# Group norm sums as four column tiles, the inverse's two products interleaved, and one block's attention pushed later

## The chip, the cores and the metric

One core of a Trainium2 chip runs the kernel. The metric is device time in microseconds (us), the median of three runs. TensorE (PE in the profile) does the matrix products, VectorE (DVE) and ScalarE (ACT) the elementwise work, GpSimd (POOL) a few fills; SyncE's queue (SP) starts nearly all transfers.

## What is computed

One layer of a decoder over 2048 prompt tokens and 64 sample tokens, width 1024. Two branches read the same normed input: sliding-window attention, and an RWKV-7 time mixer with a 64x64 state per head. Their outputs are gated, summed and projected, and a convolutional FFN follows. The two pieces that matter here:

```python
# per head of 64 channels, at every token
mean = jnp.mean(y, axis=-1, keepdims=True)
var = jnp.mean(jnp.square(y - mean), axis=-1, keepdims=True)
y = (y - mean) * lax.rsqrt(var + LNX_EPS)
...
sa = jnp.einsum('bhij,bhj->bhi', S, at)
S = S * wt[:, :, None, :] + sa[..., None] * bt[:, :, None, :] + vt[..., None] * kt[:, :, None, :]
```

The second is a recurrence over tokens. The kernel does it in chunks of 64 tokens; inside a chunk a unit triangular 64x64 system is solved, for which `inverse` builds the inverse of its matrix out of 32x32 blocks: the two diagonal blocks by substitution on VectorE, the corner block by two products, first `g`, then `g` times a diagonal block.

## The kernel before

The 2112 tokens are cut into three blocks of 704, and each block into two halves of 384 and 320 tokens. For each block: the input projection (with preparation of the recurrence), attention, inverses, chunk recurrence with group norm, then `branches` (the two output projections), `merge` (the mixing projection and the sum of squares of the next norm), and `ffn_stage`. The projection of all three blocks comes first, then branches, merge and FFN of block 0, of block 1 and of block 2.

All the large products go through `mm3` (L348 to L355): float32 values are split into a high and a low part, and three float32r products of 128x128 weights with 384 or 320 columns are added up. Below, one such product is called a *wide product*. Before every third wide product `mm3` calls `tick`, which may run one step of a background generator. The generators stand in named queues; queue "c" holds attention, inverses, chunks (recurrence and group norm) and the gathering of the branch inputs (`gather`), strictly one after the other. A generator yields how long its next step should wait, by costs written into the kernel (`cost`, `account`). `drain("c")` runs what is left in the queue. Within all this a list scheduler of the compiler still moves instructions on an engine; the rows of the section on the change show what it made of them. PE runs its instructions in that order.

The queue's contents before: attention of block 0 during the projection of block 0, inverses of block 0 during that of block 1, chunks of block 0 during that of block 2. Then

```python
self.push("c", self.attention(1), self.attention(2), self.inverses(1), self.chunks(1))
```

at branches, merge and FFN of block 0 (L1702), and inverses and chunks of block 2 at those of block 1 (L1729 to L1730), each with a drain at the end of the FFN. Sample attention belongs to block 2's.

At a group norm (`groupnorm`, L1237) four tiles `y` (two heads of 64 channels each, 384 tokens) are centred by L367, squared into `gsq`, and `headsum` (L997) sums the squares per head: twelve products (four tiles, three groups of 128 tokens), each with 128x128 squares as the weights and a two-column constant as the moving operand, so that each gives two columns. Every float32 product is two records of the trace. `merge` ends with a norm over channels: `rowsums` (L416, one-column products), a few small VectorE steps (L423, L375 to L380), and three transposes (L1037 on `nwyd`), emitted at the latest after the first 24 wide products of the FFN.

Of the kernel before, what the change touches and what calls it, by code (L numbers as in the profile page):

```python
# [14 lines left out]
ALU = mybir.AluOpType  # L15
# [15 lines left out]
LNX = 64e-5  # L31
# [12 lines left out]

CST = {}
_n = 0
for _name, _w in (("ident", 128), ("maskp", 128), ("sel", 2), ("selm", 2), ("ones", 1), ("bm", 8),
                  ("cj", 128), ("blk", 128), ("m65", 390), ("att", 256), ("masks", 128), ("m65s", 332)):
    CST[_name] = (_n, _w)
    _n += _w  # L50
# [3 lines left out]
def constants():  # L54
    c = np.zeros((P, NCST), np.float32)

    def put(name, a):
        o, w = CST[name]
        c[:, o:o + w] = a

    i = np.arange(P)
    put("ident", np.eye(P))
    s, t = i[:, None] % 64, i[None, :] % 64
    late = (i[None, :] >= 64)
    causal = np.where(late, s <= t, s < t)
    put("maskp", causal)
    put("masks", causal & (s // 8 == t // 8))
    head = (i[:, None] // 64 == np.arange(2)[None, :])
    put("sel", head)
    put("selm", head / 64.0)  # L70
    put("ones", 1.0)
    same = (i[:, None] // 64 == i[None, :] // 64)
    put("cj", np.eye(P) - same / 64.0)
    put("blk", same)
    d = 128 + i[:, None] - np.arange(256)[None, :]
    put("att", np.where((d >= 0) & (d <= 128), 0.0, NEG))
    m = np.ones(390, np.float32)
# [23 lines left out]
class Kernel:  # L101
# [892 lines left out]
            return self.tp.tile([P, 2, 384], F32, tag="xv", name="kt", bufs=2)[:].rearrange("p a c -> p (a c)")[:, :512].rearrange("p (c j) -> p c j", j=128)  # L994
        return pp.tile([P, 4, 128], F32, tag="m", name=name, bufs=2)

    def headsum(self, sq, sel, least, eps, k):  # L997

        nc = self.nc
        nt = 3 * len(sq)  # L1000
        ps = self.bank(k)
        for t in range(nt):
            nc.tensor.matmul(ps[:, 2 * t:2 * t + 2], sq[t // 3][:, t % 3 * 128:(t % 3 + 1) * 128], self.cst(sel),  # L1003
                             start=True, stop=True)
        m = self.small(2 * nt, "hsm" + k)
        if eps is None:
            nc.vector.tensor_scalar(m, ps[:, :2 * nt], least, None, op0=ALU.max)
        else:
            nc.vector.tensor_scalar(m, ps[:, :2 * nt], eps, None, op0=ALU.add)
        return self.rsqrt(m, 2 * nt, k)  # L1010

    def headrow(self, rb, r, t0):
# [6 lines left out]
    def keynorm(self, p, xk, pp):  # L1019

        nc = self.nc
        sq = [self.ntmp("nsq") for _ in HALF]
        for t, (c0, n) in zip(sq, HALF):
            nc.scalar.activation(t[:, :n], xk[:, c0:c0 + n], ACT.Square, scale=self.par("k_k", p))
        nc.gpsimd.memset(sq[1][:, HALF[1][1]:], 1.0)
        yield 0.2
        r = self.headsum(sq, "sel", 1e-24, None, "r")
        rb = pp.tile([P, 6, 128], F32, tag="rbk", name="rbk", bufs=2)
        self.headrow(rb, r, 0)
        yield 0.2  # L1030
        self.rbk[p] = rb
# [8 lines left out]
    def inverse(self, b, hf, ip):  # L1040


        nc = self.nc
        nch = HALF[hf][1] // 64
        ns = 4 * nch

        def blocks(rows, r, cols):
            for p in range(4):
                nc.sync.dma_start(t0[rows, p * nch:(p + 1) * nch],
                                  self.md[b][hf][:nch, rows, p, r, cols].rearrange("c q j -> q c j"))  # L1050

# [24 lines left out]
        q = ip.tile([P, 32, 64], F32, tag="qi", name="qinv")  # L1076
        t1 = ip.tile([P, 32, 32], F32, tag="nb", name="t1")
        nc.vector.transpose(t1[:].rearrange("p b i -> p i b"), qb[:].rearrange("p t i -> p i t"))
        yield
        nc.vector.transpose(q[:, :, 32:].rearrange("p b t -> p t b"), qb)  # L1080
        for r in range(2):
            o = 64 - r * 64
            nc.scalar.copy(q[o:o + 32, :ns, :32], q[o:o + 32, :ns, 32:])
            nc.gpsimd.memset(q[o + 32:o + 64, :, 0:32], 0.0)
        g = ip.tile([P, 24, 32], F32, tag="qb", name="g")
        yield 0.3
        for u in range(0, ns, 16):
            k = min(16, ns - u)
            ps = self.bank()
            for c in range(k):  # L1090
                for r in range(2):
                    o = 64 - r * 64
                    nc.tensor.matmul(ps[o + 32:o + 64, c * 32:(c + 1) * 32], n12[o:o + 32, u + c], t1[o:o + 32, u + c],
                                     start=True, stop=True)
            for r in range(2):
                rows = slice(96 - r * 64, 128 - r * 64)
                nc.scalar.copy(g[rows, u:u + k].rearrange("p c j -> p (c j)"), ps[rows, :k * 32])
            yield 0.2
            ps = self.bank()
            for c in range(k):  # L1100
                for r in range(2):
                    o = 64 - r * 64
                    nc.tensor.matmul(ps[o:o + 32, c * 32:(c + 1) * 32], g[o + 32:o + 64, u + c],
                                     q[o + 32:o + 64, u + c, 32:64], start=True, stop=True)
            for r in range(2):
                rows = slice(64 - r * 64, 96 - r * 64)
                nc.scalar.copy(q[rows, u:u + k, 32:64], ps[rows, :k * 32].rearrange("p (c j) -> p c j", j=32))
            yield
        for p in range(4):
            nc.sync.dma_start(self.qqd[b][hf][:nch, :, p].rearrange("c q j -> q c j"), q[:, p * nch:(p + 1) * nch])  # L1110

# [125 lines left out]
    def groupnorm(self, b, hf, y, kp, gup, gs):  # L1237

        nc = self.nc
        c0, n = HALF[hf]  # L1240
        sq = kp.tile([P, 4, 384], F32, tag="gsq", name="gsq", bufs=1)
# [4 lines left out]
        t, ready = part(0)  # L1246
        for p in range(4):
            nxt = part(p + 1) if bufs == 2 and p < 3 else None
            yield (ready,)
            ps = self.spread("cj", t, n, "c")  # L1250
# [3 lines left out]
            if p < 3:  # L1254
                yield (0.0,)
                t, ready = nxt or part(p + 1)
        yield (last,)
        r = self.headsum([sq[:, p] for p in range(4)], "selm", None, LNX, "c")

        def row(p):  # L1260
            rb = kp.tile([P, 3, 128], F32, tag="grb", name="grb", bufs=bufs)
# [6 lines left out]
        for p in range(4):  # L1268
# [6 lines left out]
            ps = self.bank("c")  # L1275
# [351 lines left out]
    def attention(self, b):  # L1627
        with self.pool("att", side="right") as ap:
            yield from self.attn_prompt(b, ap)
            if b == NB - 1:  # L1630
                yield from self.attn_sample(ap)

    def inverses(self, b):
        with self.pool("inv", side="right") as ip:
            for hf in range(2):
                yield from self.together((1.4, [self.inverse(b, hf, ip)]))
# [35 lines left out]
    def run(self):  # L1672
        self.sts, self.ols = {}, deque()
        HOLD = 4
        hs = ExitStack()
# [19 lines left out]
        with self.pool("gt") as gp:  # L1695
# [3 lines left out]
            self.drain("c")  # L1699
            lp[0].__exit__(None, None, None)  # L1700
            hs.close()
            self.push("c", self.attention(1), self.attention(2), self.inverses(1), self.chunks(1))  # L1702
            with self.pool("ms") as mp:
                ms = self.bigtile(mp, "o")
                self.branches(0, os_, ms, gts, x)
# [1 line left out]
        for b in (1, 2):  # L1707
# [16 lines left out]
            with ExitStack() as ms_:  # L1724
                mp = old if b == 2 else ms_.enter_context(self.pool("ms"))
                ms = self.bigtile(mp, "o")
                self.branches(b, os_, ms, gts, x)
                gp.__exit__(None, None, None)
                if b == 1:  # L1729
                    self.push("c", self.inverses(2), self.chunks(2))  # L1730
                xs = self.merge(b, x, ms, xp, op)
        self.ffn_stage(2, *xs, old)
        es.close()
# [83 lines left out]
```

## Time and profile before

| | us |
|---|---|
| median of 3 runs (3223.59 to 3227.27) | 3224.35 |
| the profiled execution, its own time | 3225.91 |
| span of the profiled execution | 3224.1 |
| PE busy in the span | 3195.1 (99%) |
| DVE busy | 2033.0 (63%) |
| ACT busy | 1216.3 (38%) |

The span runs from the first to the last instruction; some 1.8 us of the execution lie around it. The profiled execution is 1.56 us above the median. Starts of matmul records are measured, their ends are modelled; so a stretch on PE is best read from the start of its first record to the start of what follows.

### The profile page before, as it was taken

What the parts mean: (1) busy time and instruction counts of PE and PEld (TensorE: products, weight loads), DVE (VectorE), ACT (ScalarE), POOL (GpSimd) and SP (SyncE); (2) the same over time, 40 slices, a digit from 0 to 9 for tenths busy, and PEclk for the clock granted to TensorE, in tenths of its full rate; (3) what the DMA queues carried; (4) which work ended last, traced back from release to release, by engine and by line L of the source; (5) the groups of instructions that cost most, each with busy time, mean ns of one, the idle gap of its engine ahead of it and who ended that gap; (6) DMA issues with size and microseconds to landing.
All of it is one profiled execution on the core that took longest, in us unless ns stands there. A gap on an engine that the chain in (4) does not pass through costs nothing.

```text
span 3224.1 us, 60163 instructions
## 1 busy us (share of the span) xinstructions
PE 3195.1 (99%) x24072; PEld 3082.8 (96%) x24072; DVE 2033.0 (63%) x4601; ACT 1216.3 (38%) x2272; POOL 34.7 (1%) x99
## 2 busy tenths in 40 slices
PE   8999999999999999999999999999999999999998
PEld 8999999999999998899999999999999999999998
DVE  7676677745655576677555678855566575555556
ACT  4455433343323575633222333332223333222232
POOL 0000000000000000000000000000000000000000
PEclk9999999999999999999999999999999999999999
DMA  4644454545655633322443373253324362212222
GB/s 154 190 140 127 131 160 142 145 139 163 189 178 169 219 108 99 97 74 79 137 130 123 115 237 110 76 176 114 115 72 134 112 215 83 72 66 73 66 71 73
DMA packets 335464, 408.79 MB, mean 127 GB/s; under 512 B 110928, under 2 KB 261456, under 8 KB 334928
## 3 DMA queue, kind: packets, MB, share of 16 engines
q1 hardware_dynamic: 330576, 399.17, 39.7%
q10 hardware_dynamic: 4608, 5.77, 0.5%
q8 instruction: 189, 3.10, 0.4%
q14 instruction: 91, 0.75, 0.1%
HBM read 307.41 MB, written 98.41 MB: 126 GB/s over the span
## 4 chain that ended last, share of the span: by engine, by line
PE 82%; issue 16%; DVE 1%; DMA 0%; ACT 0%; POOL 0%; SPq 0%; POOLq 0%; DVEq 0%
PE psd L354 70%; PE psr L976 2%; PE psr L679 1%; PE psr L727 1%; PE psr L714 1%; PE psc L1184 1%; PE psr L866 1%; PE psc L1144 1%; PE psc L1177 1%; PE psc L1003 0%; PE psr L1003 0%; PE psr L964 0%; PE psc L1187 0%; PE psc L1276 0%; PE psr L354 0%
## 5 line engine op out<-in xcount | busy, mean ns | idle before, releaser
L354 PE MATMUL psd<-o,wp 128*128 128x320 f32 (+1 forms) x8736 | 1457.4, 325 | 1.3 <-DVE x L1458 1.0
L354 PEld LDWEIGHTS psd<-o,wp 128*128 128x128 f32 x8736 | 1404.4, 188 | 14.0 <-issue 4.2
L354 PE MATMUL psd<-h,wp 128*128 128x320 f32 (+1 forms) x5112 | 895.4, 328 | 11.2 <-ACT wp L340 7.7
L354 PEld LDWEIGHTS psd<-h,wp 128*128 128x128 f32 x5112 | 824.8, 189 | 23.5 <-ACT wp L340 7.7
L340 ACT CAST wp<-wr 128x1024 fp32r<-128x1024 f32 x350 | 366.9, 1048 | 602.9 <-PE psd L354 567.6
L341 DVE TENSOR_TENSOR wp<-wr,wp 128x1024 fp32r<-128x1024 f32 x350 | 428.1, 1223 | 166.8 <-ACT wp L340 161.0
L354 PE MATMUL psd<-ff,wp 128*128 128x320 f32 (+1 forms) x2880 | 489.1, 327 | 2.1 <-DVE up L1423 1.2
L354 PEld LDWEIGHTS psd<-ff,wp 128*128 128x128 f32 x2880 | 468.0, 189 | 7.7 <-issue 1.6
L1458 DVE TENSOR_TENSOR x<-x,psd 128x384 f32<-128x384 f32 (+1 forms) x288 | 148.0, 519 | 204.4 <-PE psd L354 203.5
L1430 DVE TENSOR_TENSOR gb<-psd,rb 128x64 f32<-128x64 f32 (+2 forms) x154 | 70.6, 471 | 194.9 <-PE psd L354 192.4
L1431 ACT ACTIVATE cc<-gb,pt 128x64 f32<-128x64 f32 (+2 forms) x154 | 95.6, 636 | 181.9 <-DVE gb L1430 180.3
L1433 DVE SCALAR_TENSOR_TENSOR cc<-gb,pt,cc 128x704 f32<-128x704 f32 (+1 forms) x132 | 122.0, 924 | 2.7 <-ACT cc L1431 2.0
L1442 ACT ACTIVATE cc<-cc 128x704 f32<-128x704 f32 x66 | 52.3, 793 | 142.8 <-DVE cc L1433 88.2
L1423 DVE TENSOR_TENSOR up<-psd,rb 128x384 f32<-128x384 f32 (+1 forms) x132 | 68.9, 522 | 50.4 <-PE psd L354 49.9
L1294 ACT ACTIVATE g<-psd,der 128x384 f32<-128x384 f32 (+1 forms) x64 | 35.4, 554 | 150.0 <-PE psd L354 98.7
L345 ACT CAST ff<-cc 128x384 fp32r<-128x384 f32 (+1 forms) x128 | 62.1, 486 | 61.0 <-DVE cc L1445 60.6
L346 DVE TENSOR_TENSOR ff<-cc,ff 128x384 fp32r<-128x384 f32 (+1 forms) x128 | 66.6, 521 | 28.4 <-ACT ff L345 27.9
L622 ACT ACTIVATE s<-s,nm 128x256 f32<-128x256 f32 (+2 forms) x136 | 65.8, 486 | 39.7 <-DVE nm L617 37.5
L1445 DVE TENSOR_TENSOR cc<-cc,up 128x384 f32<-128x384 f32 (+1 forms) x132 | 68.9, 524 | 14.9 <-ACT cc L1442 11.4
L821 ACT ACTIVATE xs<-psd,der 128x384 f32<-128x384 f32 (+1 forms) x56 | 31.1, 556 | 117.4 <-PE psd L354 117.4
L1355 DVE SCALAR_TENSOR_TENSOR m<-gt,psd 128x384 f32<-128x384 f32 (+1 forms) x96 | 49.6, 519 | 34.2 <-PE psd L354 33.2
L395 DVE TENSOR_TENSOR acc<-acc,sq 128x384 f32<-128x384 f32 (+1 forms) x126 | 65.4, 519 | 7.3 <-ACT sq L394 5.9
(266 smaller groups left out, 2803.5 us busy)
## 6 DMA issues: line engine op xcount, KB each, us to landing
wr<-in_w_fi SPq DMA_DIRECT2D x132, 512.0 KB, 3.5
wr<-in_w_in SPq DMA_DIRECT2D x108, 512.0 KB, 3.8
wr<-in_w_fo SPq DMA_DIRECT2D x66, 512.0 KB, 3.6
cm<-md SPq DMA_DIRECT2D x33, 512.0 KB, 5.0
gt<-gd SPq DMA_DIRECT2D x48, 352.0 KB, 3.9
md<-m SPq DMA_DIRECT2D x48, 256.0 KB, 2.8
wr<-in_w_br SPq DMA_DIRECT2D x24, 512.0 KB, 4.3
wr<-in_w_out SPq DMA_DIRECT2D x24, 512.0 KB, 3.8
```

The lines of the kernel that those rows point to most:

```text
L340: nc.scalar.copy(w[:, 0], raw)
L341: nc.vector.tensor_tensor(w[:, 1], raw, w[:, 0].bitcast(F32), op=ALU.subtract)
L346: self.nc.vector.tensor_tensor(lo, src, hi.bitcast(F32), op=ALU.subtract)
L354: nc.tensor.matmul(ps[:, :n], w[:, a, wk * 128:(wk + 1) * 128], act[:, k0 + k, b, c0:c0 + n], start=(start and k == 0 and j == 0), stop=(s ...
L395: self.nc.vector.tensor_tensor(acc, acc, sq[:, :n], op=ALU.add)
L622: nc.scalar.activation(s[:nq, h, :nk], s[:nq, h, :nk], ACT.Exp, bias=nm[:nq, h:h + 1], scale=0.125, accum_out=rs[:nq, h:h + 1])
L1423: nc.vector.tensor_tensor(up[:, c0:c0 + n], ps[:, :n], rb[:, c0:c0 + n], op=ALU.mult)
L1430: nc.vector.tensor_tensor(dst, view(ps, 0), view(rb, c0), op=ALU.mult)
L1431: nc.scalar.activation(view(c, c0), dst, ACT.Identity, bias=self.par("cb", f), scale=cw[2])
L1433: nc.vector.scalar_tensor_tensor(c[:, :npr], gb[:, u:u + npr], cw[u], c[:, :npr], op0=ALU.mult, op1=ALU.add)
L1445: nc.vector.tensor_tensor(cv, cv, up[:, c0:c0 + n], op=ALU.mult)
L1458: nc.vector.tensor_tensor(xv, xv, ps[:, :n], op=ALU.add)
```

## The change

Three edits. The group norm's sum of squares becomes four products, one for each tile, with the constant (repeated to 32 columns) as the weights and 384 columns of squares moving, into four groups of 32 PSUM partitions; ScalarE copies the sums, three transposes bring them back to token rows, and one VectorE operation picks the columns. The inverse's two products, done in pieces of 16 blocks one after the other, are cut into three pieces and interleaved so that the second product of a piece stands between products of the first of the next piece, on other rows and columns of the array. Attention of block 2 is pushed at the branches of block 1, ahead of the inverses and chunks of block 2, and the tile pool of the gates is closed from the queue behind it.

```diff
-put("selm", head / 64.0)
+put("selm", np.tile(head / 64.0, 16))
...
-        r = self.headsum([sq[:, p] for p in range(4)], "selm", None, LNX, "c")
+        ps = self.bank("c")
+        for p in range(4):
+            nc.tensor.matmul(ps[32 * p:32 * p + 32, :384], self.cst("selm"), sq[:, p], start=True, stop=True)
+        hs = self.ntmp("hs")
+        nc.scalar.copy(hs, ps[:, :384])
+        yield 0.2
+        ps = self.bank("c")
+        for t in range(3):
+            nc.tensor.transpose(ps[:, t * 128:(t + 1) * 128], hs[:, t * 128:(t + 1) * 128], self.cst("ident"))
+        m = self.small(24, "hsmc")
+        nc.vector.tensor_scalar(m[:].rearrange("q (p t h) -> q t p h", t=3, h=2),
+                                ps[:, :384].rearrange("q (t p m) -> q t p m", t=3, p=4)[:, :, :, :2], LNX, None, op0=ALU.add)
+        r = self.rsqrt(m, 24, "c")
...
-        for u in range(0, ns, 16):
...
+        cuts = [round(ns * k / 3) for k in range(4)]
+        for k in range(4):
+            first = (cuts[k], cuts[k + 1] - cuts[k], self.bank()) if k < 3 else None
+            psb = self.bank() if second else None
+            for c in range(8):
+                for r in range(2):
+                    o = 64 - r * 64
+                    if second and c < second[1]:
+                        u = second[0] + c
+                        nc.tensor.matmul(psb[o:o + 32, c * 32:(c + 1) * 32], g[o + 32:o + 64, u], q[o + 32:o + 64, u, 32:64],
+                                         start=True, stop=True)
...
+                        nc.tensor.matmul(first[2][o + 32:o + 64, c * 32:(c + 1) * 32], n12[o:o + 32, u], t1[o:o + 32, u],
+                                         start=True, stop=True)
...
-            self.push("c", self.attention(1), self.attention(2), self.inverses(1), self.chunks(1))
+            self.push("c", self.attention(1), self.inverses(1), self.chunks(1))
...
+                if b == 1:
+                    self.push("c", self.attention(2))
                 self.branches(b, os_, ms, gts, x)
-                gp.__exit__(None, None, None)
                 if b == 1:
-                    self.push("c", self.inverses(2), self.chunks(2))
+                    self.push("c", self.closed(gp), self.inverses(2), self.chunks(2))
```

How PE's instructions stand, at three places. First the sums of a group norm, in block 0's first half. L354 are wide products, `gsq` the squares, L1037 transposes (L1034 in the changed file). Before:

```order
L354 MATMUL psd<-h,wp 128x384 x7
L354 MATMUL psd<-h,wp 128x320 x12
L1003 MATMUL psc<-ct,gsq 128x2 x12
L354 MATMUL psd<-h,wp 128x320 x9
L1037 MATMUL psr<-ct,rbk 128x128 x3
```

Now:

```order
L354 MATMUL psd<-h,wp 128x384 x6
L354 MATMUL psd<-h,wp 128x320 x12
L1266 MATMUL psc<-gsq,ct 32x384 x3
L354 MATMUL psd<-h,wp 128x320 x3
L1266 MATMUL psc<-gsq,ct 32x384
L354 MATMUL psd<-h,wp 128x320 x9
L1034 MATMUL psr<-ct,rbk 128x128 x3
L354 MATMUL psd<-h,wp 128x384 x11
L1272 MATMUL psc<-ct,hs 128x128 x3
```

The twelve products of two columns are gone; three of the four tiles stand together, the fourth behind three wide products, and the transposes of the sums follow 23 wide products later. One of the six group norms has all four together, three have 3 and 1, and the two of block 2 have 2, 1 and 1.

Second the inverse, the first half of block 1's (the name `t_…,n_…` is the first product, `qinv,g` the second). Before, in block 2, which has the same pattern:

```order
L1093 MATMUL psr<-t_22661,n_21974 32x32 x32
L354 MATMUL psd<-o,wp 128x384 x9
L354 MATMUL psd<-o,wp 128x320 x14
L1103 MATMUL psr<-qinv,g 32x32
L1093 MATMUL psr<-t_22661,n_21974 32x32 x2
L1103 MATMUL psr<-qinv,g 32x32 x31
L1093 MATMUL psr<-t_22661,n_21974 32x32 x14
L354 MATMUL psd<-o,wp 128x320 x10
```

Now, the end of block 1's first half:

```order
L1096 MATMUL psr<-qinv,g 32x32 x2
L1102 MATMUL psr<-t_15137,n_14469 32x32 x2
L354 MATMUL psd<-ff,wp 128x320 x9
L354 MATMUL psd<-ff,wp 128x384 x12
L354 MATMUL psd<-ff,wp 128x320 x3
L1096 MATMUL psr<-qinv,g 32x32
L354 MATMUL psd<-ff,wp 128x320
L1096 MATMUL psr<-qinv,g 32x32 x15
```

Pairs of both products now alternate (the first two rows, eight times over in a piece), and the last piece of the second product stands alone, its first product cut off by a wide product. Of stretches of 32x32 products between wide or other full-array products there are 24 before and 37 now, in all six halves; the sums, none of which was on a part of the array before, make 13; all stretches of products on a part of the array are 266 before and 286 now.

Third the end of `merge` of block 0 (L416 are the sums over channels, `nwyd` the transposes behind VectorE's steps, L679, L714 and L727 attention). Before:

```order
L354 MATMUL psd<-o,wp 128x384 x15
L727 MATMUL psr<-pT,v 64x256 x2
L416 MATMUL psr<-ct,acc 128x1 x3
L727 MATMUL psr<-pT,v 64x256 x2
L679 MATMUL psr<-k_14610,q_14609 128x256 x8
L1037 MATMUL psr<-ct,nwyd 128x128 x3
L416 MATMUL psr<-ct,acc 128x1 x3
L714 MATMUL psr<-ct,s 128x128 x8
L354 MATMUL psd<-o,wp 128x320 x24
```

Now:

```order
L354 MATMUL psd<-o,wp 128x384 x18
L416 MATMUL psr<-ct,acc 128x1 x3
L354 MATMUL psd<-o,wp 128x384 x6
L354 MATMUL psd<-o,wp 128x320 x24
L354 MATMUL psd<-o,wp 128x384 x24
L1034 MATMUL psr<-ct,nwyd 128x128 x3
L416 MATMUL psr<-ct,acc 128x1 x3
L354 MATMUL psd<-o,wp 128x320 x24
```

Between the first sums and the transposes that need them there was no wide product, and there are 54 now. At the same place of block 1 there are 46 now; behind the transposes stand the 32 score products of the sample attention. The last product of a group norm stood 194 wide products ahead of the end of block 0's FFN, and in block 1's FFN it now stands 251 ahead.

## Rows read from the trace of the kernel before

**Rows 1.** The page: busy time, share of the span and instructions of each engine.

```profile
PE 3195.1 (99%) x24072; PEld 3082.8 (96%) x24072; DVE 2033.0 (63%) x4601; ACT 1216.3 (38%) x2272; POOL 34.7 (1%) x99
```

**Rows 2.** Timeline of PE, wide products alone: start, time, engine, what, count.

```profile
1064.72 19.47 PE L354 MATMUL psd<-h,wp 128*128 128x384 f32 x122
```

**Rows 3.** Timeline of PE around one group norm's sums.

```profile
1008.65 2.73 PE L1003 MATMUL psc<-ct,gsq 128*128 128x2 f32 x24
1011.24 6.00 PE L354 MATMUL psd<-h,wp 128*128 128x320 f32 x27
```

**Rows 4.** Windows: length; PE, PEld, DVE, ACT, POOL busy; granted clock, DMA share, GB/s.

```profile
1009.20:1012.59 3.39, 3.39 (x29) 3.39 (x29) 3.15 (x14) 0.00 (x0) 0.00 (x0) 1.00 0.52 158
1012.59:1016.00 3.41, 3.41 (x14) 3.41 (x13) 1.90 (x9) 0.68 (x2) 0.00 (x0) 0.50 0.02 5
1268.59:1272.00 3.41, 3.40 (x14) 3.41 (x15) 3.10 (x14) 2.77 (x6) 0.00 (x0) 0.50 0.00 0
1688.43:1695.25 6.82, 6.82 (x26) 6.82 (x27) 3.39 (x15) 0.00 (x0) 0.44 (x2) 0.50 0.00 0
2228.00:2233.00 5.00, 5.00 (x41) 5.00 (x40) 0.76 (x3) 2.05 (x4) 0.00 (x0) 1.00 0.00 0
```

**Rows 5.** Timeline of PE, the sums of block 2's first half.

```profile
2228.52 1.84 PE L1003 MATMUL psc<-ct,gsq 128*128 128x2 f32 x16
...
2232.32 0.72 PE L1003 MATMUL psc<-ct,gsq 128*128 128x2 f32 x6
```

**Rows 6.** Timeline of PE, stretches of the inverse's products: two records, and sixty.

```profile
572.85 0.24 PE L1103 MATMUL psr<-qinv,g 32*32 32x32 f32 x2
573.03 0.62 PE L354 MATMUL psd<-h,wp 128*128 128x384 f32 x2
573.57 1.19 PE L1103 MATMUL psr<-qinv,g 32*32 32x32 f32 x62
...
1561.38 1.14 PE L1093 MATMUL psr<-t,n 32*32 32x32 f32 x60
1562.45 4.15 PE L354 MATMUL psd<-ff,wp 128*128 128x320 f32 x24
1566.53 0.21 PE L1103 MATMUL psr<-qinv,g 32*32 32x32 f32 x1
```

**Rows 7.** Windows (length; PE, PEld; clock; DMA) of L1144 twice, then L1149.

```profile
823.90:826.00 2.10, 0.69 (x16) 0.56 (x16) 1.00 0.24 76
869.90:871.20 1.30, 0.68 (x16) 0.54 (x16) 1.00 0.08 24
...
823.90:826.00 2.10, 0.68 (x16) 0.55 (x16) 1.00 0.24 76
```

**Rows 8.** Timeline of PE, products on half of the columns, and full-array transposes.

```profile
814.84 0.69 PE L1184 MATMUL psc<-cvu,ckb 128*64 128x64 f32 x16
815.35 0.64 PE L1187 MATMUL psc<-cm,cvu 128*64 128x64 f32 x16
815.92 0.45 PE L354 MATMUL psd<-h,wp 128*128 128x384 f32 x1
...
1130.36 1.04 PE L714 MATMUL psr<-ct,s 128*128 128x128 f32 x8
1131.15 1.65 PE L354 MATMUL psd<-o,wp 128*128 128x320 f32 x9
```

**Rows 9.** Groups by line: a float32 product of 384 columns on the full array.

```profile
L1276 PE MATMUL psc<-gs,gup 128*128 128x384 f32 (+1 forms) x48 | 18.2, 461 | 0.0
```

**Rows 10.** Timeline of PE at the end of block 0's merge, then of its FFN.

```profile
1266.92 0.51 PE L1037 MATMUL psr<-ct,nwyd 128*128 128x128 f32 x3 [2.30 <-DVE nwyd L380]
...
1849.27 0.79 PE L354 MATMUL psd<-ff,wp 128*128 128x384 f32 x3 [1.21 <-DVE up L1423]
1850.28 0.80 PE L354 MATMUL psd<-ff,wp 128*128 128x384 f32 x3 [0.22 <-ACT ff L345]
1851.74 1.32 PE L354 MATMUL psd<-ff,wp 128*128 128x384 f32 x6 [0.67 <-DVE ff L346]
```

More of the change, by code (lines that the diff above doesn't have):

```diff
@@ L46 @@
 _n = 0
-for _name, _w in (("ident", 128), ("maskp", 128), ("sel", 2), ("selm", 2), ("ones", 1), ("bm", 8),
+for _name, _w in (("ident", 128), ("maskp", 128), ("sel", 2), ("selm", 32), ("ones", 1), ("bm", 8),
                   ("cj", 128), ("blk", 128), ("m65", 390), ("att", 256), ("masks", 128), ("m65s", 332)):
@@ L995, in mtile, with headsum @@
         return pp.tile([P, 4, 128], F32, tag="m", name=name, bufs=2)
-    def headsum(self, sq, sel, least, eps, k):
+    def headsum(self, sq, sel, least, k):
         nc = self.nc
@@ L1005, in headsum @@
         m = self.small(2 * nt, "hsm" + k)
[L1006 to L1009, printed above, removed]
+        nc.vector.tensor_scalar(m, ps[:, :2 * nt], least, None, op0=ALU.max)
         return self.rsqrt(m, 2 * nt, k)
@@ L1026, in keynorm @@
         yield 0.2
-        r = self.headsum(sq, "sel", 1e-24, None, "r")
+        r = self.headsum(sq, "sel", 1e-24, "r")
         rb = pp.tile([P, 6, 128], F32, tag="rbk", name="rbk", bufs=2)
@@ L1086, in inverse @@
         yield 0.3
-        for u in range(0, ns, 16):
-            k = min(16, ns - u)
-            ps = self.bank()
-            for c in range(k):
+        first = second = None
+        cuts = [round(ns * k / 3) for k in range(4)]
[3 more added lines that the diff above has]
+            for c in range(8):
                 for r in range(2):
                     o = 64 - r * 64
[L1093 to L1100, printed above, removed]
+                    if second and c < second[1]:
+                        u = second[0] + c
+                        nc.tensor.matmul(psb[o:o + 32, c * 32:(c + 1) * 32], g[o + 32:o + 64, u], q[o + 32:o + 64, u, 32:64],
+                                         start=True, stop=True)
@@ L1101, in inverse @@
                 for r in range(2):
                     o = 64 - r * 64
-                    nc.tensor.matmul(ps[o:o + 32, c * 32:(c + 1) * 32], g[o + 32:o + 64, u + c],
-                                     q[o + 32:o + 64, u + c, 32:64], start=True, stop=True)
+                    if first and c < first[1]:
+                        u = first[0] + c
+                        nc.tensor.matmul(first[2][o + 32:o + 64, c * 32:(c + 1) * 32], n12[o:o + 32, u], t1[o:o + 32, u],
+                                         start=True, stop=True)
@@ L1105, in inverse @@
             for r in range(2):
-                rows = slice(64 - r * 64, 96 - r * 64)
-                nc.scalar.copy(q[rows, u:u + k, 32:64], ps[rows, :k * 32].rearrange("p (c j) -> p c j", j=32))
-            yield
+                o = 64 - r * 64
+                if first:
+                    u, n, ps = first
+                    nc.scalar.copy(g[o + 32:o + 64, u:u + n].rearrange("p c j -> p (c j)"), ps[o + 32:o + 64, :n * 32])
+                if second:
+                    u, n = second[:2]
+                    nc.scalar.copy(q[o:o + 32, u:u + n, 32:64], psb[o:o + 32, :n * 32].rearrange("p (c j) -> p c j", j=32))
@@ L1109, in inverse @@
+            second = first
+            yield 0.2
         for p in range(4):
@@ L1257, in groupnorm @@
         yield (last,)
-        r = self.headsum([sq[:, p] for p in range(4)], "selm", None, LNX, "c")
+        ps = self.bank("c")
[3 more added lines that the diff above has]
+        nc.scalar.copy(hs, ps[:, :384])
+        yield 0.2
+        ps = self.bank("c")
[5 more added lines that the diff above has]
+        r = self.rsqrt(m, 24, "c")
         def row(p):
@@ L1631, in attention, with closed @@
                 yield from self.attn_sample(ap)
+    @staticmethod
+    def closed(pool):
+        pool.__exit__(None, None, None)
+        yield
     def inverses(self, b):
@@ L1726, in run @@
                 ms = self.bigtile(mp, "o")
+                if b == 1:
+                    self.push("c", self.attention(2))
                 self.branches(b, os_, ms, gts, x)
-                gp.__exit__(None, None, None)
                 if b == 1:
-                    self.push("c", self.inverses(2), self.chunks(2))
+                    self.push("c", self.closed(gp), self.inverses(2), self.chunks(2))
+                else:
+                    gp.__exit__(None, None, None)
                 xs = self.merge(b, x, ms, xp, op)
```

## The prediction

> **What bounds the kernel now.** The page comes first: PE is busy for 99% of the span, DVE and ACT far less [rows 1]. A PE that is busy is not yet a PE at its peak, so the timeline of PE comes next. Where no background step stands between them, 122 wide products follow one another in 19.47 us, 0.16 us each, half of them 384 and half 320 columns wide [rows 2]; 16,992 of them make 2719 us at 0.16. The other 500 us of the span are background products standing between them, stretches at a lower clock, and a few waits. All three edits touch only those. An engine other than PE matters only where PE waits for it, and the waits are few: I found 2.30 us at the end of block 0's merge and 2.1 us at the end of its FFN [rows 10].
>
> Two prices are needed for the rest.
>
> *What a stretch on a part of the array costs.* Two records of the inverse start at 572.85, two wide products follow, and the next stretch starts at 573.57 [rows 6]: 0.72 less 2 x 0.16 is 0.40 us. Sixty records start at 1561.38, 24 wide products follow, the next stretch starts at 1566.53: 5.15 less 24 x 0.16 is 1.31 us [rows 6]. So 58 more records cost 0.91 us, 16 ns each, and every stretch has a fixed 0.37 us, however short. Full-array products don't pay it: eight transposes take 0.79 us start to start, 0.10 each [rows 8].
>
> *What the clock costs.* Sums of a group norm in one piece are 24 records from 1008.65 to 1011.24, 2.59 us [rows 3]. Soon behind them the granted clock is 0.50, that is 1.2 GHz in place of 2.4, for 3.41 us, and only 14 PE records are busy in it against 29 in the window ahead [rows 4]. This stands behind all four sums that are in one piece; three falls last 3.41 us and one 6.82 [rows 4]. The two sums of block 2 are cut into pieces by other products (16 records, then wide products, then 6) [rows 5], and the clock there stays at 1.00 [rows 4]. A fifth fall stands behind the wait at the merge's end [rows 4].
>
> **The change part by part.**
>
> *Sums of the group norm.* Removed: six times 2.6 us, 15.6. Added: 24 products of 384 columns, in 13 stretches, and 18 transposes. The trace has no product on 32 columns of the array. One on the full array is two records of 461 ns mean, end included [rows 9], 0.92 us at most; scaled by columns from the transposes it is 2 x 3 x 0.10 = 0.60 at least. I take 0.65, near the lower, since the mean counts the tail that the next product covers. Side by side, products on different parts do run at once: L1144's 16 records take 0.68 us alone and 0.69 together with L1149's 16 on the other two quarters [rows 7]. On two halves of the columns, 32 records of 64 columns take 1.08 us [rows 8], 34 ns each with the way out, where a transpose of 128 columns takes 100, 50 for 64. So a stretch of one to four tiles costs 0.65 + 0.37. Thirteen are 13.3, the transposes 1.8, together 15.1: 0.5 us won. This edit's own products win almost nothing, because five of the six group norms have their four products cut apart.
>
> The Trainium skill, "TensorE: Matmul & The Clock Gate", Part 3, says that weight loads overlap products in flight only if they differ in rows of the array, and the four tiles share all rows. By it the 24 products would run one by one; the half-column row speaks against it. The price of that stands among the rivals.
>
> The copy on ScalarE and the second wait lengthen the queue by some 2 us a group norm. The end of the queue has room for it (below), so that costs nothing; without the room it would be 2 us a block.
>
> *The inverse.* Pairs of 32x32 products take 0.032 us a product now [rows 6]. With both products side by side on four places, a piece costs what the larger of its two parts does: for 24 blocks 64 product times in place of 96, for 20 blocks 56 in place of 80, over three blocks 360 in place of 528, so 168 x 0.032 = 5.4 us won. If four places are no faster than two, 0. But 13 stretches more cost 13 x 0.37 = 4.8. Net 0.6 won, between 0.6 won and 4.8 lost. Four copies more on ScalarE are hidden, since ScalarE idles for 62% of the span [rows 1].
>
> *Other stretches.* 286 less 266 is 20, and 13 + 13 are accounted for, so six stretches fall away elsewhere by the new order: 6 x 0.37 = 2.2 at most, 0 at least if they are merely joined to others at no gain; I take 0.9. PE work in all: 0.5 + 0.6 + 0.9 = 2 us won.
>
> *The clock.* With the long runs of two-column products gone, nothing is left of the kind behind which the four falls stand. Their 17.1 us at half clock lose at most 8.5; I take 8, since a few records in them are not wide products. Lower bound 0, if the new stretches draw the clock down as well.
>
> *Attention of block 2, moved.* Its products cost the same in block 1. What counts is where PE waited. At the end of block 0's merge attention filled the place of the wide products, so PE stood for 2.30 us for the norm's VectorE steps [rows 10], and a fall of the clock of 3.41 us came behind it (1.7) [rows 4]. Now 54 wide products, 8.6 us, stand in between: 4 us won. At block 1's merge there are 46, 7.4 us, so the 2.30 don't reappear there. What is late next there is nothing that the order shows; but the transposes, six records of one-column sums and the sample attention's 32 small products stand together behind them, some 3 us without a wide product, where a fall of 1.7 could come. I put 1 us for it.
>
> At the end of block 0's FFN the gathering for block 1 collided with the last FFN steps, and PE waited 1.21 + 0.22 + 0.67 = 2.1 us [rows 10]. The queue of block 0 is shorter by an attention now, so 2 us are won there. In block 1 the queue is longer, yet its last group norm product has 251 wide products behind it, 40 us, where block 0 had 194, 31 us, and lost 2.1. So no such wait appears in block 1. Attention's loads go through the same SP queue as the weights; block 1's attention has stood in the branches of block 0 in the same way, where PE shows no wait for weights beyond the listed ones. The later closing of the gates' pool delays only the inverses behind attention.
>
> **The sum.** 2 + 8 + 4 + 2 - 1 = 15 us. The profiled execution would go from 3225.9 to 3210.9; the median of the runs shown is 1.6 below it, so 3224.35 - 15 gives 3209.4.
>
> **Rivals.**
>
> *The sums run one by one*, since the four tiles share all rows of the array: 24 x 0.65 in place of 13 x 0.65 is 7.2 us more, 3216.6. The half-column rows speak against it [rows 8]. Chance 0.10. The rule of the Trainium skill named above would bring this about.
>
> *The clock falls elsewhere*, two to four times, behind new small stretches: 1.7 each, so 3213 to 3216. The stretches are short and wide products stand near them; but their places are new. Chance 0.10.
>
> *New waits in block 1*: attention, inverses and chunks all run there, and VectorE has to serve branches as well. The gathering took some 17 us in block 0, so 23 of the 40 us are spare. A wait of 6 to 10 us gives 3215 to 3219. For it speaks the 2.1 us in block 0, against it the larger distance. Chance 0.10.
>
> *Slower:* a product on 32 of 128 columns leaves most of the array empty. If the clock fell behind every one of the 13 stretches of sums, 13 x 1.7 = 22 us would be lost, 3231.5; it decides against the change from 13 falls on. The sixty-record stretches of the inverse, emptier still, have no fall behind them: all five falls are accounted for above. Chance 0.05.
>
> **How the numbers follow.** The forecast has 0.65, with a range of its own from 3204 (all bounds of PE work won, six stretches at full price) to 3214 (interleaving wins nothing). With the first two rivals and most of the third the range of 8 in 10 is 3203 to 3219. About 0.2%, 6.4 us, is what a measurement here can tell from no change, so faster means below 3217.9. The forecast is all there, the first two rivals mostly, the third less than half: faster 0.83, same 0.12, slower 0.05.
>
> **What would show it.** Right: no half clock behind the group norms; a stretch of three sums takes as long as a stretch of one, about 1.0 us of PE; the inverse's alternating pieces take half as long per product as its first pieces; no wait at block 0's merge nor at the end of its FFN. Wrong: half clock at the new sums, three sums taking 1.9 us, or PE waiting at the end of block 1's FFN. The prediction falls if the falls of the clock stay, since they are half of the sum.

## The result and the profile after

| | us |
|---|---|
| before, median of 4 runs (3223.24 to 3227.27) | 3223.97 |
| after, median of 4 runs (3198.30 to 3201.73) | 3199.64 |
| ratio, 95% interval | 0.9928, 0.9917 to 0.9940 |
| profiled execution after: time, span | 3198.30, 3196.5 |

The change made the kernel 24.3 us faster. The forecast was 15 us faster, 3209.4, with a range that ended at 3203: the direction was right and the range missed by 3.4 us. The page shows the same picture as [rows 1], with a PE that is busy for 99% of a shorter span:

```profile
PE 3171.4 (99%) x23994; PEld 3050.3 (95%) x23994; DVE 2033.8 (64%) x4601; ACT 1213.1 (38%) x2296; POOL 34.5 (1%) x99
```

First the places where a clock fall or a wait stood before. The windows of PE behind three of the new sums (length, PE busy with its records, granted clock, DMA share, GB/s), and the last line at the end of block 0's merge, answer to [rows 4]:

```profile
886.00:893.00 7.00, 7.00 (x43) 1.00 0.22 70
1004.00:1011.00 7.00, 7.00 (x57) 1.00 0.57 176
1630.00:1637.00 7.00, 7.00 (x44) 1.00 0.25 77
1247.60:1256.60 9.00, 8.31 (x51) 1.00 0.18 51
```

The clock stays at 1.00, 2.4 GHz, up to the last 11 us (in every kernel here the last 10 to 14 are at half clock). All five falls are gone. The view of waits lists everything PE waited for; total, times, longest:

```profile
PE psd L354 <- ACT wp L340: 7.7, 1, 7.7
PE psr L1034 <- DVE nwyd L380: 2.5, 1, 2.5
PE psd L354 <- DVE xs L816: 1.7, 2, 0.9
PE psr L416 <- DVE acc L395: 1.6, 1, 1.6
PE psd L354 <- DVE gb L1448: 1.3, 2, 0.7
PE psd L354 <- DVE p L506: 1.1, 1, 1.1
PE psd L354 <- DVE x L1476: 1.0, 1, 1.0
PE psd L354 <- DVE wp L341: 0.3, 1, 0.3
```

They add up to 17.2 us; the same view of the kernel before adds up to 20.8. The 2.30 us for `nwyd` at block 0's merge and the 2.1 us at the end of its FFN [rows 10] are not in the list: its 2.5 us for `nwyd` is the wait at block 2's merge, which stood there before too. No new wait in block 1 took their place. But 1.3 of the 2.30 us come back one step later in block 0, where its FFN begins: two waits for `gb`, VectorE's first step there, which needs what the transposes bring. The first of the two on PE's timeline:

```profile
1245.97 0.49 PE L1034 MATMUL psr<-ct,nwyd 128*128 128x128 f32 x3
1246.30 0.73 PE L416 MATMUL psr<-ct,acc 128*128 128x1 f32 x6
1247.62 7.63 PE L354 MATMUL psd<-o,wp 128*128 128x320 f32 x46 [0.59 <-DVE gb L1448]
```

Then the two things the change does on the array. PE's timeline at two group norms' sums:

```profile
884.82 0.85 PE L1266 MATMUL psc<-gsq,ct 128*32 128x384 f32 x6
885.60 0.71 PE L354 MATMUL psd<-h,wp 128*128 128x320 f32 x3
886.24 0.83 PE L1266 MATMUL psc<-gsq,ct 128*32 128x384 f32 x2
887.00 1.59 PE L354 MATMUL psd<-h,wp 128*128 128x320 f32 x9
...
1003.18 0.85 PE L1266 MATMUL psc<-gsq,ct 128*32 128x384 f32 x8
1003.96 0.96 PE L354 MATMUL psd<-h,wp 128*128 128x384 f32 x4
```

From a stretch's start to the next wide product it is 0.78 us for three tiles (six records), 0.76 for one and 0.78 for four: the tiles run side by side. Windows around two stretches of the inverse (length; PE busy with these records; clock; DMA); the first line holds the records of its first product, the others those of its second:

```profile
576.20:578.00 1.80, 0.74 (x32) 1.00 0.00 0
...
576.20:578.00 1.80, 0.72 (x32) 1.00 0.00 0
581.90:583.60 1.70, 0.69 (x32) 1.00 0.47 100
```

Sixty-four interleaved records on four places take what thirty-two on two places take, 0.7 us.

What the prediction has no term for shows in a run of wide products that no edit touches, in the last FFN: 384 of them, half of 384 and half of 320 columns, nothing between them. Timeline of PE, before:

```profile
2976.41 61.94 PE L354 MATMUL psd<-o,wp 128*128 128x384 f32 x384
```

And after:

```profile
2949.91 61.60 PE L354 MATMUL psd<-o,wp 128*128 128x384 f32 x384
```

The same instructions, 0.34 us less. From start to start, a product of 384 columns took 175.1 ns in this run and takes 173.4 now; one of 320 columns took 146.7 and takes 146.6. Some 5,300 of the 8,496 products of 384 columns have got faster, from the first projection on, where not one changed instruction has run; those of block 0's branches, of merges 0 and 1, of FFN 0 and of the down products have not.

### The profile page after: what moved, and what is told of

The parts are those of the page before. It is cut to its first block, busy times and chain, and to the rows that moved or that the text cites. A ratio compares the mean times of both kernels' runs of the same rounds, so it can differ in the third digit from the quotient of the medians.

```text
span 3196.5 us, 60033 instructions
## 1 busy us (share of the span) xinstructions
PE 3171.4 (99%) x23994; PEld 3050.3 (95%) x23994; DVE 2033.8 (64%) x4601; ACT 1213.1 (38%) x2296; POOL 34.5 (1%) x99
## 4 chain that ended last, share of the span: by engine, by line
PE 83%; issue 16%; DVE 0%; SPq 0%; DMA 0%; ACT 0%; POOL 0%; POOLq 0%; DVEq 0%
PE psd L354 70%; PE psr L976 1%; PE psr L679 1%; PE psr L727 1%; PE psr L714 1%; PE psc L1189 1%; PE psr L866 1%; PE psc L1149 1%; PE psc L1182 1%; PE psr L1003 0%; PE psc L1192 0%; PE psr L964 0%; PE psc L1294 0%; PE psr L354 0%; PE psr L1034 0%
## 5 line engine op out<-in xcount | busy, mean ns | idle before, releaser
L354 PE MATMUL psd<-o,wp 128*128 128x320 f32 (+1 forms) x8736 | 1457.6, 324 | 2.2 <-DVE gb L1448 1.3
L354 PEld LDWEIGHTS psd<-o,wp 128*128 128x128 f32 x8736 | 1398.6, 188 | 18.1 <-issue 7.6
L354 PE MATMUL psd<-h,wp 128*128 128x320 f32 (+1 forms) x5112 | 889.1, 327 | 10.9 <-ACT wp L340 7.7
L354 PEld LDWEIGHTS psd<-h,wp 128*128 128x128 f32 x5112 | 819.1, 188 | 24.4 <-ACT wp L340 7.7
L354 PE MATMUL psd<-ff,wp 128*128 128x320 f32 (+1 forms) x2880 | 483.2, 326 | 0.0
L354 PEld LDWEIGHTS psd<-ff,wp 128*128 128x128 f32 x2880 | 464.0, 188 | 6.6 <-issue 2.5
L631 DVE CUSTOM_DVE_ANT_0 s<-psr,att 128x256 f32<-128x256 f32 (+2 forms) x136 | 49.7, 404 | 27.4 <-PE psr L679 26.9
```

Source lines behind the costliest of these rows:

```text
L354: nc.tensor.matmul(ps[:, :n], w[:, a, wk * 128:(wk + 1) * 128], act[:, k0 + k, b, c0:c0 + n], start=(start and k == 0 and j == 0), stop=(s ...
```

## The experiments

**The theory for the wide products** (called A): the change widens the constant tile `ct` from 2 to 32 columns of `selm`. That is 120 bytes a partition, 128 with the alignment, and everything that is allocated later on the left side of SBUF (the kernel's pools take their space from both ends of it) moves up by it, the weight tiles `wp` too (48,160 to 48,288 in the compiled kernel's addresses). The activations on the right side (`h`, and `o` of blocks 1 and 2) stay. A product reads both. The distance from weight tile to moving tile, modulo 256 bytes, was 192 for nearly all; it is 64 now for right-side tiles, and still 192 for left-side ones, which move along. That is the line between the products that got faster and those that did not. Left-side activations and weights both moved by 128 bytes and kept their pace (175.3 ns before and 175.4 after in the down products of FFN 0 and 1), so it would be the distance that counts, and not the place of either. The rivals are the execution or the chip, and the new order of work.

**Unused columns in the constant tile.** Four kernels, three from the kernel before and one from the changed one, with this line changed (16 and 48 for 32 in the third and fourth) and no instruction but the constant's own load:

```diff
-for _name, _w in (("ident", 128), ("maskp", 128), ("sel", 2), ("selm", 2), ("ones", 1), ("bm", 8),
+for _name, _w in (("ident", 128), ("maskp", 128), ("sel", 2), ("selm", 2), ("ones", 1), ("bm", 8), ("pad", 32),
```

> The kernel before with 32 unused columns at the end of its constant tile and nothing else: every tile that the left side allocates after the constants, the weight tiles among them, moves up by 128 bytes, while the activation tiles on the right side stay. Theory A (the pace of the 384-column products hangs on how far the moving tile stands from the weight tile): 384-column products in the first projections, branches 1 and 2, merge 2 and the first halves of feed-forwards 1 and 2 go from 174.9 to 175.2 ns each to about 173.3 ns; all five clock falls stay; time 3216 us, 3213 to 3219. Theory B (the pace differs from run to run or from chip to chip): no change of pace that the kernel before does not show too, 3223 to 3225 us. A third theory (the pace comes from the order of work in the changed kernel): as B.

> The changed kernel with 32 more unused columns in the constant tile, so that the weight tiles stand 256 bytes above where they stand in the kernel before, a multiple of 256. Theory A: the 384-column products go back to 174.6 to 175.2 ns and the time to about 3207.5 us (3206 to 3210), 8 us above the changed kernel; there are still no clock falls. Theories B and order of work: as the changed kernel, 3198 to 3202 us.

> The kernel before with 16 unused columns: the weight tiles move by 64 bytes. Theory A, if the place modulo 256 bytes decides: the products of the right-side tiles then stand as those of the second half of feed-forward 2 do now (176.1 ns), so about +1 ns for each of some 5400 products: slower by 3 to 6 us, 3227 to 3230. Theory B: 3223 to 3225.

> The kernel before with 48 unused columns: the weight tiles move by 192 bytes, to a distance of 0 modulo 256 that no tile of the kernel before or of the changed kernel has. Theory A says only that the pace depends on it: another mean than 174.9 ns is to be expected, in either direction (3215 to 3230). Theory B: 3223 to 3225.

Measured (before: 3223.36):

| kernel | distance of `o` in the last FFN | us | ratio to before, 95% |
|---|---|---|---|
| before + 32 | 64 | 3214.06 | 0.9972 (0.9960 to 0.9984) |
| after + 32 | 192 | 3207.74 | 0.9951 (0.9938 to 0.9963) |
| before + 16 | 128 | 3228.83 | 1.0016 (1.0007 to 1.0025) |
| before + 48 | 0 | 3217.71 | 0.9982 (0.9973 to 0.9991) |

All four came where A put them; for the fourth A's range was so wide that only the pace of the products tells. The run of 384 products in the last FFN on PE's timeline, before + 32:

```profile
2965.12 61.60 PE L354 MATMUL psd<-o,wp 128*128 128x384 f32 x384
```

After + 32:

```profile
2958.99 61.94 PE L354 MATMUL psd<-o,wp 128*128 128x384 f32 x384
```

Before + 16:

```profile
2980.53 62.11 PE L354 MATMUL psd<-o,wp 128*128 128x384 f32 x384
```

Before + 48:

```profile
2968.02 61.74 PE L354 MATMUL psd<-o,wp 128*128 128x384 f32 x384
```

Read by distance: 64 is fastest, 0 costs 0.14 us more, 192 0.34, 128 0.51. (The second half of FFN 2's down products stands at 128 in the kernel before and in the changed one, and takes 176.1 ns in both.) The two kernels at 64 agree to the hundredth, and so do the two at 192, though one of each has the old order and one the new: order and execution are out, and so is the chip, since the later kernels, run on two others, show 61.94 us at 192 and 61.60 at 64 again. The changed kernel with the old distance takes 3207.74, so of its 24 us 8.1 are the place of the tiles and some 15.6 the three edits, where 15 were forecast.

The Trainium skill, "SBUF — State Buffer", section "SBUF: two separate sides", says that on the engines' side only the port pair shared by VectorE and GpSimd causes contention, and its section "A bandwidth-pool intuition that's wrong (but worth ruling out)" gives PE a second, independent read port for weights. Neither passage gives the place of a tile a part in the pace. It has one here, 0.5 us in 62; what inside the chip does it no run shows.

**One edit at a time.** The sums alone (padded to 256 bytes, so at the old pace), the inverse alone, the moved attention alone:

> The group norm sums of the change alone, on the kernel before; its widened constant tile is padded by 32 more columns, so that the weight tiles stand 256 bytes off, where the 384-column products keep the pace of the kernel before. By the prediction's terms: four clock falls behind the sums go (-8 us), the fall and the wait at block 0's merge stay, sums and transposes win 0.5: 3214.9 us, 3213 to 3216.5. Rival, the falls belong to the place and not to the two-column products: 3222 to 3224, with four falls still there. Rival, tiles one after another: about +7 us on the first.

> The interleaved inverse alone, on the kernel before. By the prediction's term 0.6 us won: 3222.8 us, five clock falls as before. If the part of the PE work that was under-estimated (2 us forecast, some 4.4 read from the changed kernel's trace) lies here, 3220 to 3221. If interleaving wins nothing and the stretches cost their price, 3226 to 3228.

> The moved attention alone, on the kernel before. By the prediction's terms: 2.3 us of wait and a fall of 1.7 us at block 0's merge, 2.1 us of waits at the end of feed-forward 0: 6 us won, less the allowance of 1: 3217.4 to 3218.4 us; four clock falls behind the sums stay. Rival, the waits come back in block 1: 3221 to 3223.

And the sums and the inverse together, without the move:

> The changed sums and the interleaved inverse, attention where it was before, weights 256 bytes off (the slow pace of before). If the parts add up: 3223.5 - 2.5 - 2.1 = 3218.9 us. If the sums' new waits at feed-forward 0's end are what the moved attention removes, the same 3218 to 3219, with some 3 us of waits there, and the rest of the difference to 3207.7 belongs to the move. If the sums and the inverse help each other without it: 3213 to 3216.

Measured (before: 3223.52, and 3223.14 for the last): 3220.97 (0.9991, 0.9982 to 1.0000), 3221.42 (0.9992, 0.9984 to 1.0001), 3217.52 (0.9980, 0.9971 to 0.9989), and 3223.02 (1.0002, 0.9993 to 1.0011). The time of the attention came as forecast. The sums alone win 2.5 us where 8.6 were forecast, and with the inverse they win nothing, which none of the three expectations had. Taken apart by profile: "clock" is half of the time at 0.50, without the end; "waits" the total of the view of waits; "rest" what is left of the span. Each row is one execution; that of before lies 2.4 us above the median of 3223.52.

| profiled execution | span | clock | waits | rest |
|---|---|---|---|---|
| before | 3224.1 | 10.2 | 20.8 | 3193.1 |
| sums | 3219.1 | 3.4 | 24.0 | 3191.7 |
| inverse | 3221.0 | 8.5 | 21.2 | 3191.3 |
| attention | 3215.4 | 3.4 | 18.8 | 3193.2 |
| sums + inverse | 3221.2 | 6.8 | 27.5 | 3186.9 |
| all three, old distance | 3206.4 | 0.0 | 18.5 | 3187.9 |
| all three (the change) | 3196.5 | 0.0 | 17.2 | 3179.3 |

The sums and the inverse do their work: 6.2 us less of it, and no fall behind a group norm. They lose it elsewhere. Timeline of PE of sums + inverse: the last product of block 0's group norms, then the end of FFN 0, with the wait in brackets:

```profile
1835.75 0.70 PE L1294 MATMUL psc<-gs,gup 128*128 128x320 f32 x2
...
1850.91 5.65 PE L354 MATMUL psd<-o,wp 128*128 128x384 f32 x28 [0.88 <-DVE x L1476]
...
1860.73 2.56 PE L354 MATMUL psd<-o,wp 128*128 128x384 f32 x6 [3.06 <-ACT o L345]
1866.90 0.63 PE L354 MATMUL psd<-o,wp 128*128 128x320 f32 x1 [3.61 <-DVE m L1373]
```

And the window over it:

```profile
1860.70:1870.90 10.20, 6.56 (x20) 5.67 (x21) 4.79 (x10) 2.13 (x5) 0.00 (x0) 0.50 0.67 241
```

The same two places in the kernel before:

```profile
1830.62 0.70 PE L1276 MATMUL psc<-gs,gup 128*128 128x320 f32 x2
...
1866.14 4.08 PE L354 MATMUL psd<-o,wp 128*128 128x384 f32 x22
```

Block 0's queue gets there 5 us later (each group norm has a copy and a wait more), while block 1's branches begin 15 us earlier, since PE has come through with less work and fewer falls. Of some 35 us between the two 15 are left. The branches wait for their gathered `o` (3.06 us), then for VectorE's step with the gates (3.61), and a fall of 10.2 us stands there. The moved attention takes work out of just that queue: with it the waits fall from 27.5 to 18.5 and the clock stays up, 15.3 us between 3223.02 and 3207.74, against 6.0 alone. Those 6.0 are not the terms of the forecast, either: its waits are 2.0 us shorter and not 4.4, and two of the four falls behind sums, which it does not touch, were absent in its profiled execution.

**What draws the clock down.** The sums as before, but cut, in two ways, and the change with the long runs put back. First, each three of a group norm's twelve sums held back until wide products stood behind the three before:

> The kernel before with its two-column sums as they are, but each group norm's twelve products cut into four threes with wide products between them (3 to 24 of them), begun 3 us later. Theory, a long run of two-column products draws the clock down: the four falls behind the sums go without a wide product on part of the array, -8 us, 3215 us (3213 to 3218, since the order around them moves too). Rival, two-column products draw it down however spread: four falls stay, 3222 to 3225.

It took 3286.90 us (1.0196, 1.0182 to 1.0209) and decides nothing: holding back made the queues late, and PE stood where they are emptied.

```profile
PE psc L372 <- ACT parts L347: 14.7, 13, 1.7
```

That line of its view of waits (total, times, longest) is the largest of the new ones; half-clock stretches of up to 20 us lie around them. So the second cut moves nothing and puts filling products between, four after every three:

```diff
...
+            if k % 3 == 2 and k < 11:
+                for u in range(4):
+                    nc.tensor.matmul(ps[:, 128:128 + n], self.cr["cj"], t[:, u % 2, :n], start=True, stop=True)
...
```

> The kernel before with its two-column sums unchanged, but after every third of a group norm's twelve products four wide products stand whose result nobody reads (36 of 384 and 36 of 320 columns in all: 36 x 0.174 + 36 x 0.146 = 11.5 us of added work). Theory, the run of two-column products without a wide one draws the clock down: no fall behind a group norm's sums (at most the one at the merge and one near feed-forward 0's end are left), so 11.5 less 4 to 7: 3228 to 3231 us. Rival, the falls have nothing to do with the run's length: falls stay, 3235 us.

And in the changed kernel, behind the three transposes:

```diff
+        for k in range(12):
+            nc.tensor.matmul(ps[:, 384 + 2 * k:386 + 2 * k], hs[:, k % 3 * 128:(k % 3 + 1) * 128], self.cst("sel"),
+                             start=True, stop=True)
```

> The changed kernel with twelve two-column products back behind each group norm's transposes, whose results nobody reads: 6 x 2.6 = 15.6 us of added work. Theory, such a run draws the clock down: falls stand behind some of the six again, 1.7 us each, 3218 to 3223 us, and the times spread over several us. Rival, the changed kernel's falls went for another reason: 3215.2 us, tight, and a clock of 1.00 behind every run.

With fillers, 3237.75 us (1.0046, 1.0033 to 1.0059), some 7 us above the upper end of what was expected. Yet the theory's own mark is there. The timeline of PE in one of its norms:

```profile
1009.15 0.72 PE L1260 MATMUL psc<-ct,gsq 128*128 128x2 f32 x6
1009.73 0.83 PE L1264 MATMUL psc<-parts,cjr 128*128 128x320 f32 x4
1010.40 0.72 PE L1260 MATMUL psc<-ct,gsq 128*128 128x2 f32 x6
```

And the window over it (length; PE, PEld, DVE, ACT, POOL; granted clock):

```profile
1005.00:1025.00 20.00, 20.00 (x134) 19.10 (x133) 13.08 (x41) 6.01 (x14) 0.00 (x0) 1.00 0.47 141
```

No fall behind any of its sums. The two falls left, 6.83 us each, stand at the wait at block 0's merge and at one of 2.7 us at FFN 0's end; its rest is 11.5 us above before, the fillers' price. These two falls, twice as long as most, give back most of what the four at the sums won, and longer waits at that end of the queue, priced at nothing, cost 1.8: 9.9 us between the two profiled executions. The medians lie 14.6 apart; what the 4.7 more are no trace shows.

With the runs back, 3223.43 us (1.0003, 0.9994 to 1.0012), just above the 3218 to 3223 expected and between 3220.6 and 3226.6: 23.8 us above the changed kernel for work that adds 18.6 to the rest. Four of the six runs have a fall behind them; one run on PE's timeline:

```profile
1648.17 3.18 PE L1274 MATMUL psc<-ct,hs 128*128 128x2 f32 x24
```

And the windows of two of the falls, the second behind that run:

```profile
1012.00:1015.41 3.41, 3.41 (x13) 0.50 0.34 135
1650.33:1657.16 6.83, 6.83 (x27) 0.50 0.01 2
```

Counted over the profiles of the seven kernels that have such runs (before, before + 32, + 16, + 48, inverse, attention, runs back), 19 of 29 uninterrupted runs of 24 two-column records have a fall behind them, 71.7 us of half clock, a loss of 1.2 us a run on average. None stands behind the 30 sums on column tiles (five kernels), the 6 with fillers, or 9 runs of 16 records; one stands behind a run of 18. (The kernel whose sums were held back is left out, since its falls stand among waits.) Which runs are hit changes from kernel to kernel with the same instructions there: before has 4 of 4, before + 32 2 of 4.

**The rest of the tiles.** By A the left-side activations are still at the slow distance. A pool of 128 unused bytes behind the weight tiles moves what lies behind it on that side and nothing else:

```diff
         self.wp = pool("wsplit", 2)
+        pool("pad", 1).tile([P, 32], F32, name="pad")
```

> The changed kernel with a pool of 128 unused bytes between the weight tiles and the activation tiles that lie behind them on the left side. Their distance from the weights was the slow one before and after; now it is that of the fast right-side tiles. Theory A: some 2,500 products of 384 columns in branch 0, merges 0 and 1, feed-forward 0 and the down products of feed-forwards 0 and 1 go from about 175 to 173.3 ns: 4 to 5 us off the changed kernel, 3195 us (3194 to 3196.5). If the distance of the left-side tiles does not matter: 3199 to 3201.

3194.42 us (0.9913, 0.9900 to 0.9927; before 3223.14), 3193.87 to 3194.84: as expected, 5.2 us below the changed kernel, and the fastest here. The down products of its FFNs (L355 is L354 in the others), for which the changed kernel's row reads 281.0 us:

```profile
L355 PE MATMUL psd<-ff,wp 128*128 128x384 f32 x1440 | 278.6, 338 | 0.0
```

## Why the prediction was off, step by step

**"All three edits touch only those"**: this step failed. The prediction left the 2719 us of wide products out of the sum because no edit changes them. One edit changes where their weights lie. That is worth 8.1 us, by the change with and without 32 unused columns, as much as the largest term of the sum, the clock's 8. Without it the three edits make 15.6 us by median, and the kernel with the old distance lies at 3207.74, inside the range of 3203 to 3219. The groups by line show it; first the change at the old distance:

```profile
L354 PE MATMUL psd<-o,wp 128*128 128x384 f32 x4368 | 821.1, 339 | 0.0
L354 PE MATMUL psd<-h,wp 128*128 128x384 f32 x2568 | 501.8, 342 | 8.6 <-ACT wp L340 8.1 <-DVE wp L341 0.5
```

And the change as it is:

```profile
L354 PE MATMUL psd<-o,wp 128*128 128x384 f32 x4368 | 817.1, 339 | 0.0
L354 PE MATMUL psd<-h,wp 128*128 128x384 f32 x2568 | 498.2, 341 | 8.0 <-ACT wp L340 7.7 <-DVE wp L341 0.3
```

4.0 and 3.6 us less, on 384-column products alone. So the range was left because of a term put at nothing. Its lower end was not well founded, either: all bounds of PE work won, as it says, are 0.65 us of the sums' products and 1.3 of the other stretches, which gives 3207.4 and not 3204.

**The clock, 8 and 1.7.** The mechanism held: long runs of two-column products draw the clock down, and a fall stands at the merge's wait wherever that wait is. (Whether the wait alone draws it, or the small products beside it too, is not shown.) The size came from one execution with four falls of four [rows 4]. At the mean of 1.2 us a run four runs cost 4.9. The fall at block 0's merge was there in all eight profiles with the attention in its old place whose queues were not held back (2.3 us lost on average), and there was one more near FFN 0's end in two of the five of these that have the order before or the inverse alone. Together that is about 8 of the 9.7 forecast. A fall seen once in a trace is a chance, and its price a mean.

**Work on PE, 2.** Too small: the rest is 5.2 us lower at the old distance. The prices behind the sums were right: a stretch of sums costs 0.98 us where 1.02 were taken (from 884.82 to 886.24 it is 1.42, less three wide products of 0.146), and four places work at once in the inverse. Alone the two edits win 1.4 and 1.8 where 0.5 and 0.6 were forecast; together 6.2. What the 3 us that only the two together win consist of stays open: stretches on a part of the array, the one cost that was counted ahead, don't fall in number with both (in the traces 290 before, 306 with both, and 309 in the changed kernel).

**Sums one by one**, the rival at 0.10 that the Trainium skill's rule in "TensorE: Matmul & The Clock Gate", Part 3, would bring: it didn't come. Four tiles that share all rows take 0.78 us, one 0.76. The same page of the Trainium skill, section "Why this matters for your kernels", has column groups running concurrently, and the rows agree with that.

**"The end of the queue has room", and the attention, 4 and 2.** Right for the path, too large for the waits: the 4.4 us of them [rows 10] are gone, but 1.3 came back as waits for `gb` where FFN 0 begins, and at the old distance 0.7 in block 1's branches. In all the waits fall by 2.3 us there (20.8 to 18.5). And the two sentences are one. The room is made by the move. Without it the sums and the inverse cost not the 2 us a block that the prediction named but 6.7 us of waits and a fall of 10.2 us, all that they had won.

**The allowance of 1, new waits, and the slower rival**: in the change as it is none came in block 1. At its merge the clock stays up and no wait is listed.

**The sum without the place of the tiles.** 5.2 of work, 8 of the clock and 2.3 of waits are 15.5, next to 15.6 measured and 15 forecast. That the forecast of the three edits came so near is in part luck: 3.2 us too little for the work and an allowance of 1 that was not needed stood against some 1.7 too much for the clock and 2 for the waits.

## What to carry to other kernels

An edit that resizes a constant can change the pace of products that it does not touch: when allocations move, compare a long run of untouched products in both traces before pricing anything else, and try a few paddings; 128 bytes a partition gave 5 us more here. Edits that share a queue are not priced one by one: work saved by two was lost at the queue's late end until the third shortened it. And a price read from rare events in one profiled execution needs their frequency over several.

## What was not expected of the hardware

The pace of a 384-column product depends on how far its moving tile lies from its weight tile modulo 256 bytes: over 192 such products 61.60 us at 64, 61.74 at 0, 61.94 at 192, 62.11 at 128 (with 192 products of 320 columns in between, whose pace differs by 0.4 ns at most). From start to start that is 173.4, 174.4, 175.1 and 176.1 ns a product of 384 columns. With the same instructions the clock fell behind two runs of two-column products in three, not behind each. The Trainium skill's "TensorE: Matmul & The Clock Gate", Part 1, "What's actually happening", says that the moments at which the chip decides on the clock don't follow the kernel's start. The runs agree with that: 4 falls of 4 in one profile and 2 of 4 in another, behind the same instructions.
